# Half of the softmax tiles of a hybrid encoder block turned by VectorE and DMA instead of TensorE, with the source's order on all engines

## The chip, the cores and the metric

One core of a Trainium2 chip runs the kernel. The metric is the device time of one execution in microseconds; lower is better. The engines are TensorE (PE, matrix products; PEld is its loading of weights), VectorE (DVE), ScalarE (ACT), GpSimd (POOL) and SyncE (SP), which here only issues DMAs. DMAs can also be issued from ScalarE's queue. On-chip data lie in SBUF with 128 partitions; TensorE writes to PSUM, from where VectorE or ScalarE read.

## The reference

One layer over 512 positions of width 2048:

- `mod = silu(c) @ w_cond + b_cond` gives shift, scale and gate; `h = rms_norm(x) * (1 + scale) + shift`.
- `proj = h @ w_in` (7200 columns) is cut into attention queries, keys, values and gate (1024 each), the queries, keys, values and gate of a gated linear attention (512, 512, 1024, 1024) and two low-rank gates (16 each).
- Attention: 16 heads of width 64, three dilated window patterns whose outputs are merged with weights from their softmax denominators:

```
s = einsum(q, k) / 8 + bias[bucket]; s = where(mask, s, -1e30)
p = exp(s - max); den = sum(p); o = (p / den) @ v; lse = max + log(den)
att = sum over patterns of softmax(lse) * o
```

- Linear attention: 4 heads, chunked scans forward and backward, summed, normalised.
- `y = concat(att * silu(gate_a), gla * silu(gate_g)) @ w_out`; the result is `rms_norm(x + gate * y) * final_gain`.

## The kernel before

Everything is float32. A product is made exact enough by splitting both sides into a high and a low part (float32r) and summing three products: `three(ps, lh, ll, rh, rl)` issues high × high, low × high, high × low, each a matmul of 128×128 by 512 columns. The three dilated patterns are one softmax over all 512 keys: a row of biases per head (`grow`, in DRAM) holds the T5 bias plus the log of how many patterns see a distance.

After a start that computes `h` and the first products, the kernel runs **units**: qk2, qk4, qk6, gk, gv0, gv1, ag0, ag1, gg0, gg1, o0 to o3. A unit makes 512 columns of a projection: 8 weight groups g (two 128-row blocks of 512 columns each, one DMA of 512 KB), and in each group four output tiles of two products, so 64 **ticks** of `three`. Its four accumulators (`PJ`) come from five PSUM buffers; three more (`PA`) serve everything else. The weights of a group are loaded into one of four `raw` buffers (`fetch`), split by ScalarE into a high part (`split_hi`) and by VectorE into a low part (`split_lo`); three buffers hold each part. At the start of a group, the code splits the next group and fetches two ahead; `upto` says how far.

Between the ticks a unit carries **side work**, a list of (position from 0 to 1, function). A position of 1 or more is carried into the next unit. For qk2, qk4, qk6 and gk it is attention over two pairs of heads (`attention(pairs)`), 16 tiles of 128 queries each:

- `score(h, i)`: two matmuls make 128 queries × 512 keys in PSUM; VectorE adds the bias and takes the minimum, ScalarE exponentiates with the sum, VectorE inverts the sum, GpSimd scales: the tile `p`.
- `turn(h, i)`: TensorE transposes `p` in four 128×128 blocks into PSUM; ScalarE takes the high part, VectorE the low one.
- `values(h, half)`: eight matmuls with the turned tiles of two `i`; ScalarE and VectorE put the two rows of sums together in `cat`.

At the end of qk2, qk4 and qk6, `qk_evict` reads the four finished accumulators for the two pairs of heads that the next unit will need: per pair four ScalarE and four VectorE instructions and four DMAs on SP that copy keys to the other 64 partitions.

Further side work are the **sums** (`some_sums`): 48 loads of 512 KB and VectorE reductions over them for the gate and for a bias; `SUMS_IN` says how many each unit carries.

TensorE runs in the source's order throughout (`tc.manual_schedule(engines={E.PE})`). In the start, the other engines run in an order planned by `_plan` (with `manual_schedule(engines=PLANNED)`, where PLANNED are GpSimd, VectorE, ScalarE and SyncE). In all units after it the tile scheduler orders those four engines; side work is marked a little more urgent (`urgent`, an offset of 20).

Of the kernel before, what the change touches and what calls it, by code (L numbers as in the profile page):

```python
# [72 lines left out]
ATT_AT = (0.17, 0.8, 0.04, 0.05, 0.05)  # L73
# [4 lines left out]
SUMS_IN = {"qk6": 4, "gk": 4, "gv0": 9, "gv1": 2, "ag0": 7, "ag1": 9, "gg0": 9}  # L78
# [55 lines left out]
def block_kernel(ctx: ExitStack, tc: tile.TileContext, a: dict):  # L134
# [421 lines left out]
    def attention(pairs):  # L556

        tiles = [(2 * p + j, i) for p in pairs for j in range(2) for i in range(4)]
        gt, pt, pr_ = {}, {}, {}
        heads = [2 * p + j for p in pairs for j in range(2)]  # L560

        def g_load(h):
            g = gp.tile([P, 896], F32, tag="g", name=f"g{h}")
            nc.sync.dma_start(g, bass.AP(grow.tensor, grow.offset + h * 1024, [[1, P], [1, 896]]))
            gt[h] = g

        def score(h, i):
            def go():
                if h % 8 == 0 and i == 0:
                    cat[h // 8] = B8(f"cat{h // 8}", [4, 512])  # L570
# [12 lines left out]
                act(t, t, AF.Exp, bias=st[:, 0:1], scale=-1.0, accum_out=st[:, 1:2])  # L583
                nc.vector.reciprocal(st[:, 2:3], st[:, 1:2])  # L584
# [4 lines left out]
        def turn(h, i):  # L589
            def go():  # L590
# [7 lines left out]
                hi = pt[h, half][:, 0, :, P * ii:P * ii + P]  # L598
                lo = pt[h, half][:, 1, :, P * ii:P * ii + P]
# [4 lines left out]

        def values(h, half):
            def go():
                t = pt.pop((h, half))
# [15 lines left out]
        for x in range(n + 4):  # L623
            if x < n:
                items.append(score(*tiles[x]))
            if 2 <= x <= n + 1:
                items.append(turn(*tiles[x - 2]))
            if 3 <= x <= n + 2 and tiles[x - 3][1] % 2 == 1:
                items.append(values(tiles[x - 3][0], tiles[x - 3][1] // 2))
        g_load(heads[0])  # L630
        start, span, move0, move1, move_last = ATT_AT
        at = [start + (q + 0.5) / len(items) * span for q in range(len(items))]
        at[0] -= move0
        at[1] -= move1
        at[-1] += move_last
        return list(zip(at, items))
# [206 lines left out]
    def unit(name, natural, side=(), rhs=None, lr=None, tiles=range(4)):  # L843
# [5 lines left out]
        for q in range(KT // 2):  # L849
            g = gorder[q] if name == "o3" else q  # L850
            i0 = gi[name, g]
            todo = []
            if 0 in tiles:
                todo = list(range(gi[name, gorder[0] if name == "o3" else 0], upto[name, g] + 1))
# [4 lines left out]
            if i0 not in low:  # L859
                split_lo(i0)  # L860
            hi, lo = wts[i0]
            for n, i in enumerate(tiles):
                for kk in range(2):
                    k = 2 * g + kk
                    rh, rl = (h_hi[:, k, :], h_lo[:, k, :]) if rhs is None else rhs[k]
                    if natural:
                        t = slice(i * P, i * P + P)
                        cw = slice(kk * 512, kk * 512 + 512)
                        three(ps[n], rh[:, t], rl[:, t], hi[:, cw], lo[:, cw], q + kk == 0, q + kk == KT // 2)
                    else:  # L870
                        c = slice(kk * 512 + i * P, kk * 512 + i * P + P)
                        three(ps[n], hi[:, c], lo[:, c], rh, rl, q + kk == 0, q + kk == KT // 2)
                    tick += 1
                    if tick % (2 * len(tiles)) == 2:
                        for i_ in todo:
                            split_lo(i_)
                    while pos < len(side) and side[pos][0] * ticks <= tick:
                        urgent(side[pos][1])
                        pos += 1
                if lr is not None:  # L880
                    lr(4 * g + i)
# [18 lines left out]
    for p in range(2):  # L900
        qk_evict(p, psb["b", 4 + 2 * p], psb["b", 5 + 2 * p])
    for n, p in (("qk2", 0), ("qk4", 2), ("qk6", 4)):
        ps = unit(n, False, attention((p, p + 1)) + ([(0.05, shift_row)] + some_sums(n) if p == 4 else []))
        for q in range(2):
            qk_evict(p + 2 + q, ps[2 * q], ps[2 * q + 1])

    ps = unit("gk", False, attention((6, 7)) + some_sums("gk"))
    gla["k"] = B8("gkt", [4, 512])
    for i in range(4):
        act(gla["k"][:, i, :], ps[i], AF.Copy)  # L910


    lrb = B8("lrb", [KT, 32])
    nc.sync.dma_start(lrb, a["w_lr"][0])
    lrs = B8("lrs", [KT, 2, 32], F32R)
    act(lrs[:, :, 0, :], lrb, AF.Copy)
    tt(lrs[:, :, 1, :], lrb, lrs[:, :, 0, :].bitcast(F32), op=ALU.subtract)
    plr = PA("plr")

    def lr_tick(n):  # L920
        if n % 2 == 1:
            k = n // 2
            w = lrs[:, k, :, :].rearrange("p a b -> p (a b)")
# [207 lines left out]
```

## Time and profile before

| | us |
|---|---|
| median of 3 runs | 958.9 (958.15 to 960.98) |
| the profiled execution | 959.9 |
| its span, first to last instruction | 957.9 |
| TensorE busy | 939.7 (98%) |
| VectorE busy | 605.3 (63%) |
| ScalarE busy | 431.5 (45%) |
| GpSimd busy | 81.1 (8%) |

The span is what the profile sees; the profiled execution took 2.0 us more. TensorE's busy time counts a pipelined matmul from its start to its modelled end, so consecutive matmuls overlap: a 512-column matmul has 0.39 us, but the next starts 0.23 us later. The chain of waits counts each instruction only from the end of the one before. A group row gives line, engine, operation, output and inputs, shapes, count, then busy us and the mean ns of one, and the idle time of that engine ahead of these instructions with what ended it. A timeline row gives start, duration, engine, line, operation, tiles and in brackets the idle time ahead. A row of DMA issues gives the size and the median time from issue to landing.

### The profile page before, as it was taken

The numbers are of one execution on the slowest core, as the hardware profiler recorded it, in microseconds if no ns is written. First come the engines' busy times: TensorE is split into PE (matmuls) and PEld (weight loads), VectorE is DVE, ScalarE is ACT, GpSimd is POOL, SyncE is SP. The second block draws the span as 40 slices with busy tenths as digits, with TensorE's granted clock in tenths as the row PEclk, the third lists the DMA queues.
The fourth block names the chain that finished last, engine by engine and source line by source line (L and its number), as shares of the span: only waits on it lengthen the run. The fifth ranks groups of instructions, "written<-read, shape, count | busy, mean of one in ns | idle before, by whom it ended". The sixth has DMA issues, their size and how long they took to land.

```text
span 957.9 us, 11999 instructions
## 1 busy us (share of the span) xinstructions
PE 939.7 (98%) x4464; PEld 777.1 (81%) x4464; DVE 605.3 (63%) x900; ACT 431.5 (45%) x719; POOL 81.1 (8%) x100
## 2 busy tenths in 40 slices
PE   8999999999999999999999999999999999999996
PEld 5888788888888888888778888888887888888884
DVE  7988899675756676766435656675964352546421
ACT  5443533565655655655215544543834152233222
POOL 0000000012122022122000000000010000202120
PEclk9999999999999999999999999999999999999998
DMA  9999687443333463533454244354555464244013
GB/s 330 413 411 365 229 296 275 150 131 105 112 103 105 144 200 108 173 127 103 150 176 146 86 132 154 132 176 154 173 195 183 132 221 154 92 151 152 23 55 121
DMA packets 45180, 163.76 MB, mean 171 GB/s; under 512 B 5730, under 2 KB 6018, under 8 KB 40386
## 3 DMA queue, kind: packets, MB, share of 16 engines
q1 hardware_dynamic: 44946, 162.68, 49.9%
q8 instruction: 35, 0.57, 0.2%
q10 hardware_dynamic: 176, 0.33, 0.1%
q14 instruction: 23, 0.18, 0.1%
HBM read 154.51 MB, written 4.28 MB: 166 GB/s over the span
## 4 chain that ended last, share of the span: by engine, by line
PE 84%; DMA 6%; DVE 5%; issue 3%; ACT 1%; SPq 0%; POOL 0%; ACTq 0%; DVEq 0%; POOLq 0%
PE ps_o L170 6%; PE ps_o L169 6%; PE ps_o L171 6%; DMA rawg<-in_wg 6%; PE ps_qk L170 5%; PE ps_qk L169 5%; PE ps_qk L171 5%; PE o L611 3%; PE sta L169 3%; PE sta L170 3%; PE sta L171 3%; PE stb L171 3%; PE stb L169 3%; PE stb L170 3%; PE ps_gv L171 3%; PE ps_gv L170 3%
## 5 line engine op out<-in xcount | busy, mean ns | idle before, releaser
L585 POOL TENSOR_SCALAR p<-p,st 128x512 f32<-128x512 f32 x64 | 45.5, 711 | 406.6 <-DVE st L584 357.9
L244 DVE CUSTOM_DVE_ANT_0 cb<-cb,sb,c_bcond 128x2048 f32<-128x2048 f32 (+1 forms) x32 | 73.4, 2294 | 0.0
L583 ACT ACTIVATE p<-p,st 128x512 f32<-128x512 f32 x64 | 46.1, 721 | 56.8 <-DVE st L580 56.3
L602 DVE TENSOR_TENSOR pt<-t,pt 128x512 fp32r<-128x512 f32 x64 | 44.0, 689 | 16.2 <-ACT pt L601 15.8
L580 DVE CUSTOM_DVE_ANT_0 p<-s,g 128x512 f32<-128x512 f32 x64 | 43.6, 687 | 14.8 <-PE s L577 14.5
L601 ACT ACTIVATE pt<-t 128x512 fp32r<-128x512 f32 x64 | 37.8, 592 | 10.2 <-PE t L597 9.2
L244 DVE CUSTOM_DVE_ANT_0 rawg<-rawg,sb,gate 128x1024 f32<-128x1024 f32 x16 | 20.5, 1283 | 29.6 <-DMA rawg<-in_wg 29.6
L611 PEld LDWEIGHTS o<-pt,vv 128*128 128x128 f32 x256 | 34.7, 188 | 5.0 <-DVE pt L602 2.2
L597 PEld LDWEIGHTS t<-c_ident,p 128*128 128x128 f32 x256 | 31.8, 140 | 8.5
L597 PE MATMUL t<-c_ident,p 128*128 128x128 f32 x256 | 38.3, 272 | 0.0
L611 PE MATMUL o<-pt,vv 128*128 128x256 f32 x256 | 36.6, 283 | 0.9 <-DVE pt L602 0.8
L244 DVE CUSTOM_DVE_ANT_0 rawg<-rawg,sb,c_bcond 128x1024 f32<-128x1024 f32 x16 | 20.5, 1283 | 26.3 <-DMA rawg<-in_wg 26.3
L1014 POOL TENSOR_TENSOR x<-x,fgain 128x512 f32<-128x512 f32 x12 | 20.3, 1696 | 185.3 <-ACT ysq L1012 185.3
L1012 ACT ACTIVATE ysq<-x 128x512 f32<-128x512 f32 x16 | 10.1, 632 | 47.2 <-DVE x L1010 47.2
L767 POOL TENSOR_SCALAR dc<-st,sc 128x256 f32<-128x256 f32 x16 | 10.4, 652 | 245.5 <-DVE st L764 240.6
L1009 DVE TENSOR_TENSOR y<-ps_o,sb 128x512 f32<-128x512 f32 x16 | 10.9, 684 | 25.9 <-PE ps_o L171 25.9
L584 DVE RECIPROCAL st<-st 128x1 f32<-128x1 f32 x64 | 10.3, 162 | 24.9 <-ACT p L583 24.9
L576 PE MATMUL s<-ks,qs 128*128 128x512 f32 x64 | 25.1, 391 | 0.0
L577 PE MATMUL s<-kl,qs 128*128 128x512 f32 x64 | 25.0, 391 | 0.0
L774 ACT ACTIVATE sq<-st,sc 128x256 f32<-128x256 f32 x24 | 12.2, 509 | 26.8 <-DVE st L769 14.3
L1010 DVE TENSOR_TENSOR x<-y,x 128x512 f32<-128x512 f32 x16 | 18.0, 1125 | 0.3
L614 ACT ACTIVATE oh<-o 64x256 f32<-64x256 f32 x32 | 12.2, 382 | 13.0 <-PE o L611 12.2
(1275 smaller groups left out, 2916.7 us busy)
## 6 DMA issues: line engine op xcount, KB each, us to landing
cb<-in_wm SPq DMA_DIRECT2D x31, 1024.0 KB, 7.9
rawg<-in_wg SPq DMA_DIRECT2D x32, 512.0 KB, 3.4
raw_o<-in_w_o SPq DMA_DIRECT2D x32, 512.0 KB, 3.4
raw_qk<-in_w_qk SPq DMA_DIRECT2D x24, 512.0 KB, 3.4
rawb<-in_w_sb SPq DMA_DIRECT2D x16, 512.0 KB, 4.8
rawv<-in_wv SPq DMA_DIRECT2D x16, 512.0 KB, 3.8
raw_gv<-in_w_gv SPq DMA_DIRECT2D x16, 512.0 KB, 3.5
raw_ag<-in_w_ag SPq DMA_DIRECT2D x16, 512.0 KB, 3.3
```

Of the source, the lines that this page charges most:

```text
L169: mm(ps, lh, rh, start=first, stop=False)
L170: mm(ps, ll, rh, start=False, stop=False)
L171: mm(ps, lh, rl, start=False, stop=last)
L244: nc.vector.tensor_tensor_reduce(out=w, in0=w, in1=with_, op0=ALU.mult, op1=ALU.add, scale=1.0, scalar=init, accum_out=dst)
L576: mm(ps, qs[:, q], ks, start=True, stop=False)
L580: nc.vector.tensor_tensor_reduce(out=t, in0=ps, in1=gt[h][:, P * i:P * i + 512], op0=ALU.add, op1=ALU.min, scale=1.0, scalar=3e38, accum_o ...
L583: act(t, t, AF.Exp, bias=st[:, 0:1], scale=-1.0, accum_out=st[:, 1:2])
L585: nc.gpsimd.tensor_scalar(t, t, st[:, 2:3], 1.0, op0=ALU.mult, op1=ALU.mult)
L597: nc.tensor.transpose(pk[:, kt * P:kt * P + P], t[:, kt * P:kt * P + P], ident)
L601: act(hi, src, AF.Copy)
L602: tt(lo, src, hi.bitcast(F32), op=ALU.subtract)
L611: mm(po[:, :256], vv[h // 4][:, kt, h % 4, :], t[:, w, kt, :], start=kt == 0 and w == 0, stop=kt == 3 and w == 1)
```

## The change

Attention: each head has four query tiles in two halves. Half 0 (tiles 0 and 1) no longer goes to TensorE. VectorE's transpose turns the 32×32 blocks within the tile (`turn`), two DMAs store the tiles to DRAM (`leave`), four DMAs read them back so that the blocks come to lie in their places (`back`, into a `raw` buffer), and ScalarE and VectorE split the half into a high part (`part_hi`) and a low part (`part_lo`), 128×1024 each. Half 1 is turned by TensorE as before (`pe_turn`). Every step has its own position in units of tiles (`x + 1.1` and so on), spaced by `ATT_AT`; the last steps fall into the next unit.

The region from the first `qk_evict` to the end of gv0 stands in `manual_schedule(engines=PLANNED)`: ScalarE, VectorE, GpSimd and SyncE issue in the order of the source there.

In the units of q, k and gk, weights are fetched on ScalarE's queue, as are the bias tiles (`g_load`). These units handle groups 0 and 1 as one step: tile by tile, both groups. Eight sums leave qk6 and gk for gv0, gv1, ag0 and gg1. The low-rank weights are loaded and split during gk.

```diff
-ATT_AT = (0.17, 0.8, 0.04, 0.05, 0.05)
+ATT_AT = (0.12, 0.057)
+BY_DVE = (0,)
+BACK_AT = (2.7, 4.1, 4.4, 5.6)
-SUMS_IN = {"qk6": 4, "gk": 4, "gv0": 9, "gv1": 2, "ag0": 7, "ag1": 9, "gg0": 9}
+SUMS_IN = {"gv0": 12, "gv1": 5, "ag0": 8, "ag1": 9, "gg0": 9}
...
-            nc.sync.dma_start(raws[i], a["w_" + u][g])
+            queue = nc.scalar if u[:2] in ("qk", "gk") else nc.sync
+            queue.dma_start(raws[i], a["w_" + u][g])
...
+        def turn(h, i):
+            def go():
+                t = T2(f"pt{h}{i}")
+                nc.vector.transpose(t.rearrange("p (b k r) -> p k b r", b=4, k=4), pr_.pop((h, i)))
+                pr_[h, i] = t
+            return go
+        def leave(h, i):
+            def go():
+                half, ii = divmod(i, 2)
+                if ii == 0:
+                    away[h, half] = dp.tile([2, P, 512], F32, tag=f"away{h}{half}", name=f"away{h}{half}")
+                nc.sync.dma_start(away[h, half][ii], pr_.pop((h, i)))
+            return go
+        def back(h, half):
+            def go():
+                t = away.pop((h, half))
+                f = RAW(f"pf{h}{half}", [8, 128])
+                for b in range(4):
+                    nc.sync.dma_start(f[32 * b:32 * b + 32], bass.AP(
+                        t.tensor, t.offset + P * b, [[512, 32], [32 * 512, 8], [1, P]]))
+                pf[h, half] = f
+            return go
+        def part_hi(h, half):
+            def go():
+                t = pt[h, half] = B8(f"pt{h}{half}", [2, 4, 256], F32R)
+                src = pf[h, half].rearrange("p b (k r) -> p k b r", k=4)
+                act(t[:, 0].rearrange("p k (b r) -> p k b r", b=8), src, AF.Copy)
+            return go
...
+        for x in range(n):
+            h, i = tiles[x]
+            items.append((x, score(h, i)))
+            items.append((x + 0.75, scale(h, i)))
+            half, ii = divmod(i, 2)
+            if half in BY_DVE:
+                items.append((x + 1.1, turn(h, i)))
+                items.append((x + 1.5, leave(h, i)))
+                if ii:
+                    for at, piece in zip(BACK_AT, (back, part_hi, part_lo, values)):
+                        items.append((x + at, piece(h, half)))
+            else:
+                items.append((x + 1.8, pe_turn(h, i)))
+                if ii:
+                    items.append((x + 2.9, values(h, half)))
+        start, step = ATT_AT
+        return [(start + step * x, go) for x, go in items]
...
+        steps = [order_[:2]] if name[:2] in ("qk", "gk") else [order_[:1], order_[1:2]]
+        for step in steps + [[g] for g in order_[2:]]:
...
+                todo = list(range(gi[name, order_[0]], upto[name, step[-1]] + 1))
                 for i in todo:
                     split_hi(i)
                 for ahead in (1, 2):
-                    fetch(upto[name, g] + ahead)
+                    fetch(upto[name, step[-1]] + ahead)
+            for g in step:
+                split_lo(gi[name, g])
             for n, i in enumerate(tiles):
+                for g in step:
...
+    with tc.manual_schedule(engines=PLANNED):
+        for p in range(2):
+            qk_evict(p, psb["b", 4 + 2 * p], psb["b", 5 + 2 * p])
+        for n, p in (("qk2", 0), ("qk4", 2), ("qk6", 4)):
+            ps = unit(n, False, attention((p, p + 1)) + ([(0.6, shift_row)] if p == 4 else []))
+            for q in range(2):
+                qk_evict(p + 2 + q, ps[2 * q], ps[2 * q + 1])
```

More of the change, by code (lines that the diff above doesn't have):

```diff
@@ L622, in attention @@
         n = len(tiles)
[L623 to L629, printed above, removed]
-        g_load(heads[0])
[L631 to L636, printed above, removed]
+        for x in range(n):
[13 more added lines that the diff above has]
+                    items.append((x + 2.9, values(h, half)))
+        items.sort(key=lambda v: v[0])
+        g_load(heads[0])
+        start, step = ATT_AT
+        return [(start + step * x, go) for x, go in items]
     def gate_half(m, z):
@@ new lines, in unit @@
+                for g in step:
+                    hi, lo = wts[gi[name, g]]
+                    for kk in range(2):
+                        k = 2 * g + kk
+                        rh, rl = (h_hi[:, k, :], h_lo[:, k, :]) if rhs is None else rhs[k]
+                        first, last = (g, kk) == (order_[0], 0), (g, kk) == (order_[-1], 1)
+                        if natural:
+                            t = slice(i * P, i * P + P)
+                            cw = slice(kk * 512, kk * 512 + 512)
+                            three(ps[n], rh[:, t], rl[:, t], hi[:, cw], lo[:, cw], first, last)
+                        else:
+                            c = slice(kk * 512 + i * P, kk * 512 + i * P + P)
+                            three(ps[n], hi[:, c], lo[:, c], rh, rl, first, last)
+                        tick += 1
+                        if tick % (2 * len(tiles)) == 2:
+                            for i_ in todo:
+                                split_lo(i_)
+                        while pos < len(side) and side[pos][0] * ticks <= tick:
+                            urgent(side[pos][1])
+                            pos += 1
+                    if lr is not None:
+                        lr(4 * g + i)
@@ L897, in gate_evict @@
         lnexp()
[L900 to L910, printed above, removed]
```

85 lines of the change are left out of this document (39 added, 46 removed).

## The prediction

> **What bounds the kernel now.** I read the page's busy table first, then the stretches of the five projection units that the change touches, then the chain of waits inside one of them.
>
> ```profile
> span 957.9 us, 11999 instructions
> PE 939.7 (98%) x4464; PEld 777.1 (81%) x4464; DVE 605.3 (63%) x900; ACT 431.5 (45%) x719; POOL 81.1 (8%) x100
> ```
> ```profile
> 191.87:257.29 65.42, 65.39 (x345) 54.91 (x344) 43.49 (x90) 38.84 (x75) 11.15 (x16) 1.00 0.37 113
> 257.29:323.71 66.42, 66.39 (x353) 55.91 (x352) 41.95 (x89) 37.43 (x72) 11.17 (x16) 1.00 0.36 108
> 390.28:457.51 67.23, 66.39 (x353) 55.92 (x352) 45.01 (x94) 36.50 (x70) 12.05 (x16) 1.00 0.42 132
> 457.51:510.39 52.88, 52.51 (x233) 41.21 (x232) 20.14 (x26) 12.15 (x15) 0.00 (x0) 1.00 0.46 150
> ```
> The stretches are the units qk2, qk4, gk and gv0 (length, then PE, PEld, DVE, ACT, POOL busy, granted clock, DMA share, GB/s). TensorE is busy in all but 0.03 us of qk2 and of qk4, 0.84 of gk and 0.37 of gv0. So a microsecond taken from TensorE's list there is a microsecond won, and a microsecond for which TensorE waits is lost: there is no slack to hide it in.
>
> ```profile
> 204.04 0.23 PE ps_qk L171
> 204.27 0.44 PE t L597 x4
> 204.71 0.23 PE ps_qk L169
> 210.68 0.94 PE o L611 x8
> ```
> In the chain one 512-column matmul counts 0.23 us (a tick of three 0.68), four transposes 0.44, the eight matmuls of a "values" step 0.94. Unit qk2 is made of 192 × 0.2267 = 43.5, 16 scores of two matmuls 7.3, 16 turns 7.0 and 7 values 6.6 (the eighth falls into the next unit): 64.4 of the measured 65.4. The remaining 1.0 I spread over its 23 interruptions, 0.04 each.
>
> **The change part by part.**
>
> *Half of the turns leave TensorE.*
> ```profile
> L597 PE MATMUL t<-c_ident,p 128*128 128x128 f32 x256 | 38.3, 272 | 0.0
> L602 DVE TENSOR_TENSOR pt<-t,pt 128x512 fp32r<-128x512 f32 x64 | 44.0, 689 | 16.2 <-ACT pt L601 15.8
> L580 DVE CUSTOM_DVE_ANT_0 p<-s,g 128x512 f32<-128x512 f32 x64 | 43.6, 687 | 14.8 <-PE s L577 14.5
> L585 POOL TENSOR_SCALAR p<-p,st 128x512 f32<-128x512 f32 x64 | 45.5, 711 | 406.6 <-DVE st L584 357.9 <-PE t L597 16.2 <-PE s L576 10.8
> ```
> 256 transposes are 64 turns; 32 go: 32 × 0.44 = 14.1 us, and 32 × 0.04 = 1.3 of the interruptions. **−15.4**, all on the path.
>
> *What replaces them, off the path if on time.* Each of 32 tiles gets a block transpose by VectorE. No row shows one; by the nearest ones below it costs between 0.48 (128x256) and 1.22 us (a scan of 128x512); I take 0.69, the two-input 128x512 row above, since it walks the same 512 columns once.
> ```profile
> L432 DVE SCALAR_TENSOR_TENSOR vv<-vraw,rcol,vv 128x256 fp32r<-128x256 f32 x16 | 6.7, 479 | 0.0
> L717 DVE TENSOR_TENSOR_SCAN b<-rst,g 128x512 f32<-128x512 f32 x4 | 4.9, 1225 | 0.1
> L297 DVE TENSOR_TENSOR qk41l<-raw_qk,qk41h 128x1024 fp32r<-128x1024 f32 x1 | 1.2, 1222 | 0.0
> ```
> The split of 128x512 twice (2 × 0.69) becomes one of 128x1024 (1.22). Per unit VectorE gains 8 × 0.69 − 4 × 0.16 = +4.9 us: 43.5 to 48.4 in a unit of about 62. Covered at 0.69 and, at 1.22, still below the unit (52.6).
>
> *The round trip.* Per half of a head: two stores of 256 KB, then four loads of 128 KB that wait on SP for the stores.
> ```profile
> g<-grow SPq DMA_DIRECT2D x16, 448.0 KB, 4.4
> out<-x SPq DMA_DIRECT2D x16, 256.0 KB, 2.6
> ks<-ks SPq DMA_DIRECT2D x16, 128.0 KB, 2.2
> ```
> ```profile
> 256.65 0.46 SPq L549 DMA_DIRECT2D ks<-ks  x1
> ```
> One attention step is 0.057 of a unit, 3.5 us. Counted from a score: matmuls 0.45, VectorE 0.7, ScalarE 0.7, POOL 0.71 and handovers make p ready at about 3.4; VectorE turns it behind the next score's work, done at 5.6; store 2.6: 8.2. The loads go out from 2.7 steps or then, four issues of 0.46, the last landing 2.2 (like ks) to 4.4 (like g) later: 11.8 to 14.0. The high part is asked for at 4.1 steps, 14.4. Nominally on time, **0** on the path; queued behind it on SP are only the next stores and loads, since the weights of these units have moved to ScalarE's queue. The 16.8 MB go into units whose DMA share is 0.36 to 0.5.
>
> *Source's order on all engines.* This is where I see the loss. The timelines at the end of qk2 (ScalarE, then VectorE, then TensorE):
> ```profile
> 248.92 1.06 ACT L313 ACTIVATE qk41h<-raw_qk 128x1024 fp32r<-128x1024 f32 x1 [0.95 <-PE ps_qk L171]
> ...
> 256.03 0.59 ACT L548 ACTIVATE ks<-ps_qk 64x512 fp32r<-64x512 f32 x1
> 256.64 0.59 ACT L539 ACTIVATE qs<-ps_qk 64x512 fp32r<-64x512 f32 x1
> ...
> 267.00 0.72 ACT L583 ACTIVATE p<-p,st 128x512 f32<-128x512 f32 x1 [2.02 <-DVE st L580]
> ...
> 267.72 0.71 ACT L583 ACTIVATE p<-p,st 128x512 f32<-128x512 f32 x1
> ```
> ```profile
> 256.76 0.69 DVE L550 TENSOR_TENSOR kl<-ps_qk,ks 64x512 fp32r<-64x512 f32 x1
> ...
> 270.14 0.69 DVE L580 CUSTOM_DVE_ANT_0 p<-s,g 128x512 f32<-128x512 f32 x1 [1.43 <-PE s L577]
> ```
> ```profile
> 257.29 0.39 PE L169 MATMUL ps_qk<-h_hi,qk40h 128*128 128x512 f32 x1
> ...
> 263.71 0.39 PE L169 MATMUL ps_qk<-h_hi,qk41h 128*128 128x512 f32 x1
> ...
> 269.60 0.39 PE L577 MATMUL s<-kl,qs 128*128 128x512 f32 x1
> ```
> Before, group 1 of qk4 is split at 248.9, 8.4 us ahead of the unit, between the evictions, and TensorE needs it 6.4 us into the unit. After, the source emits the split of group 1 only at the new unit's start, behind `qk_evict` of both pairs; and TensorE, which now takes groups 0 and 1 tile by tile, needs it after two ticks. Let 0 be the issue end of the old unit's last matmul. The last score (step 15, 0.12 + 15 × 0.057 = 0.975, tick 63 of 64) has its second matmul at −0.91. By the rows VectorE starts 0.54 later (269.60 to 270.14), −0.37, and takes 0.70; ScalarE's exp is done 0.72 after 0.37, at 1.09. Then eight evictions 0.61 apart (256.03 to 256.64): 5.97. The high part of group 1: 7.0. VectorE's eight eviction steps of 0.69, each behind ScalarE's, end at 7.45; the low part, 1.22: 8.7. TensorE has two ticks and one turn, 1.36 + 0.44 = 1.8, issues one matmul when the high part comes, and would have started the second at 2.0: **6.7 lost**. Then the turn of tile 15 waits: VectorE does group 2's low part first (to 10.0), reciprocal, POOL 0.71: 10.9, where TensorE arrives at 10.5: 0.4. Together 7.1 at each of three borders (qk2/qk4, qk4/qk6, qk6/gk): **+21.3**. Bounds for one border: 3.5 (if only the last pair's two k evictions, 1.2, 1.4 of VectorE and the split stood behind the end) and 9 (if issuing g's load and the two fetches held ScalarE as well). At gk/gv0 there are only four evictions and group 1 isn't needed for eight ticks: nothing; the 0.84 and 0.37 us idle of gk and gv0 come from the old order there and may go: **−1.2**.
>
> *The clock.* TensorE would stand still from 1.8 to 7.0, 5.2 us. The end and the start of this trace show what that does:
> ```profile
> 948.22 0.39 PE L171 MATMUL ps_o<-o36l,c_h 128*128 128x512 f32 x1
> ```
> ```profile
> 951.00:952.00 1.00, 0.00 (x0) 0.00 (x0) 0.58 (x1) 0.94 (x3) 0.45 (x1) 1.00 0.00 0
> 952.00:953.00 1.00, 0.00 (x0) 0.00 (x0) 0.17 (x1) 0.75 (x2) 0.73 (x1) 0.65 0.00 0
> ```
> ```profile
> 12.67 0.80 PE L170 MATMUL sta<-sa0h,h_lo 128*128 128x512 f32 x1
> ...
> 15.40 0.63 PE L170 MATMUL sta<-sa0h,h_lo 128*128 128x512 f32 x1
> 15.83 0.63 PE L171 MATMUL sta<-sa0l,h_hi 128*128 128x512 f32 x1
> ```
> ```profile
> 17.32 0.39 PE L169 MATMUL sta<-sa0h,h_hi 128*128 128x512 f32 x1
> 17.55 0.40 PE L170 MATMUL sta<-sa0h,h_lo 128*128 128x512 f32 x1
> ```
> The last matmul ends at 948.6; the granted clock falls at about 952.3 (0.65 over that microsecond), 3.7 us later. At the start dense matmuls go every 0.43 us from 12.67 to about 17.0 and 0.23 after: 4.3 us at half rate, 2.0 lost. An idle time of 5.2 is above 3.7, but one observation doesn't say that it happens each time: I take two of three borders, **+4.0**, bounds 0 and 6. [...]
>
> *Sums moved.*
> ```profile
> L244 DVE CUSTOM_DVE_ANT_0 rawg<-rawg,sb,gate 128x1024 f32<-128x1024 f32 x16 | 20.5, 1283 | 29.6 <-DMA rawg<-in_wg 29.6
> ```
> Eight sums leave qk6 and gk; gv0 and gv1 get three more each, ag0 and the last gate unit one. 3 × 1.28 = 3.9 us on a VectorE busy 20 of 53 us in gv0: 0, bounds −1 and +3 (if a late load holds the weight splits behind it). The early load of the low-rank weights is in the −1.2.
>
> **Sum.** The profiled execution took 959.9 (span 957.9 and 2.0 around). 959.9 − 15.4 + 21.3 − 1.2 + 4.0 = 968.6; it stands 1.0 above the median of the three runs, 958.9, so **968**, 0.9% slower.
>
> **Rivals.**
> *The border is short (faster).* The gain is 16.6; three borders cost as much at 5.5 us each, clock included. If ScalarE and VectorE reach group 1 soon after the last tile, at 3.5 a border and no drop of the clock: 958.9 − 16.6 + 10.5 = 953; with no stall at all 942. For it: the operands are on chip in time (raw weights are fetched a whole group ahead), and ScalarE is only 56% busy (37.4 of 66.4 us). Against: the eviction of the last tile can't begin before 0, and emission order puts all eight behind the last exp.
> *About no change.* A border of 5.5, or 7.1 without the clock and with a further 3 us of spared interruptions: 956 to 962.
> *The steady state stalls as well.* In source order VectorE's list for one head (four scores 0.69, two turns, two plus one splits, weight splits 1.22 twice, merges) is 10.7 of 14 us, and each item waits for its place: the merge of one half stands behind the next tile's score, and a score's PSUM buffer (three in all) behind the merge. Decides if a head loses over 0.3 us; at 0.8 per head, 16 heads: +13, 981. For it the low slack of the round trip, 0.4 us at its slow bound. [...]
> *It does not do what it says:* TensorE's turns stay at 64. Excluded by the source, no chance given.
>
> **How the numbers follow.** Border stall as worked out 0.47 (968; own range 962 to 975), short border 0.24 (953), about no change 0.14 (959), steady stalls too 0.15 (981). A measurement of this kernel can tell about 0.3%, 2.9 us, from no change. Short border counts as faster with a part of the third case; faster 0.25, same 0.13, slower 0.62. The range 951 to 980 leaves out the no-stall end (a tenth) and the worst of the steady stalls (a tenth).
>
> **What would show it.** 32 × 4 transposes on TensorE; qk2 near 62 us, qk4, qk6 and gk near 69; TensorE idle 5 to 7 us in front of the first matmul with group 1, released by ScalarE's high part and then VectorE's low part of qk41, qk61, gk1; matmuls every 0.43 us behind some of these gaps. Wrong if those gaps are under 5 us, or if idle time is spread over the turns and values, released by part_lo or by loads of pf.

## The result: 4.0% slower, and the profile after

The changed kernel takes 998.2 us (median; 996.7 to 998.8) against 959.0 for the kernel before on the same chip: ratio 1.040, 95% interval 1.038 to 1.042. The sign and the place were forecast, the size was not: 39 us lost instead of 9, beyond the forecast's 951 to 980.

The page of the changed kernel, its span and its busy table:

```profile
span 997.0 us, 11866 instructions
PE 937.9 (94%) x4336; PEld 771.8 (77%) x4336; DVE 620.9 (62%) x917; ACT 428.1 (43%) x704; POOL 78.9 (8%) x100
```

TensorE has 128 matmuls fewer (32 × 4: the turns did leave it). It is now idle for 59 us of the span (997.0 − 937.9), against 18 before. The stretches of the units qk2, qk4, qk6, gk and gv0 (columns as in the prediction):

```profile
192.98:260.12 67.14, 62.20 (x297) 51.10 (x296) 40.24 (x83) 31.07 (x59) 9.96 (x15) 0.97 0.56 168
260.12:337.30 77.18, 66.02 (x321) 54.53 (x320) 45.49 (x93) 36.68 (x68) 11.08 (x17) 0.93 0.52 147
337.30:415.00 77.70, 66.50 (x322) 55.13 (x321) 45.49 (x93) 36.85 (x69) 11.07 (x17) 0.91 0.56 159
415.00:492.72 77.72, 66.84 (x321) 55.22 (x320) 45.53 (x93) 37.32 (x70) 10.87 (x16) 0.91 0.54 147
492.72:549.10 56.38, 54.14 (x248) 42.70 (x247) 29.81 (x43) 16.82 (x24) 1.38 (x2) 1.00 0.67 227
```

qk4 and gk, each of which begins with a border behind a qk unit, are 10.8 and 10.5 us longer than before, qk6 11.1 and qk2 1.7. The stretch given for gv0 leaves out its last two matmuls (gv1 begins at 549.56); with them gv0 is 4.0 longer. The border qk2/qk4 in the timelines of TensorE, ScalarE and VectorE:

```profile
261.49 0.60 PE L608 MATMUL t<-c_ident,p 128*128 128x128 f32 x4
270.59 0.79 PE L173 MATMUL ps_qk<-h_hi,qk41h 128*128 128x512 f32 x1 [8.50 <-ACT qk41h L318]
271.85 0.79 PE L174 MATMUL ps_qk<-h_hi,qk41l 128*128 128x512 f32 x1 [0.47 <-DVE qk41l L302]
272.44 0.63 PE L175 MATMUL ps_qk<-h_lo,qk41h 128*128 128x512 f32 x1
272.87 0.63 PE L173 MATMUL ps_qk<-h_hi,qk41h 128*128 128x512 f32 x1
...
284.97 0.36 PE L665 MATMUL o<-pt,vv 128*128 128x256 f32 x1 [1.61 <-DVE st L583]
```
```profile
261.26 0.59 ACT L544 ACTIVATE qs<-ps_qk 64x512 fp32r<-64x512 f32 x1
262.60 0.59 ACT L544 ACTIVATE qs<-ps_qk 64x512 fp32r<-64x512 f32 x1 [0.75 <-DVE qs L545]
...
264.67 0.59 ACT L553 ACTIVATE ks<-ps_qk 64x512 fp32r<-64x512 f32 x1 [0.86 <-DVE kl L555]
...
266.80 0.59 ACT L544 ACTIVATE qs<-ps_qk 64x512 fp32r<-64x512 f32 x1 [0.92 <-DVE qs L545]
...
268.86 0.59 ACT L553 ACTIVATE ks<-ps_qk 64x512 fp32r<-64x512 f32 x1 [0.86 <-DVE kl L555]
...
269.48 1.06 ACT L318 ACTIVATE qk41h<-raw_qk 128x1024 fp32r<-128x1024 f32 x1
...
281.90 1.06 ACT L647 ACTIVATE pt<-pf 128x1024 fp32r<-128x1024 f32 x1 [4.78 <-DMA pf<-away]
```
```profile
269.49 0.69 DVE L555 TENSOR_TENSOR kl<-ps_qk,ks 64x512 fp32r<-64x512 f32 x1 [0.66 <-ACT ks L553]
270.57 1.23 DVE L302 TENSOR_TENSOR qk41l<-raw_qk,qk41h 128x1024 fp32r<-128x1024 f32 x1 [0.39 <-ACT qk41h L318]
...
282.99 1.22 DVE L654 TENSOR_TENSOR pt<-pf,pt 128x1024 fp32r<-128x1024 f32 x1 [5.15 <-ACT pt L647]
284.13 0.68 DVE L583 CUSTOM_DVE_ANT_0 p<-s,g 128x512 f32<-128x512 f32 x1
```

Read from the bottom up. TensorE stops behind the turn at 261.49, as forecast; it would have gone on at 261.93 and gets the high part of group 1 at 270.59, then waits for the low part. That is 8.66 + 1.03 = 9.7 us by the starts. ScalarE comes to the split of group 1 at 269.48 because the eight evictions stand ahead of it and four of them wait for VectorE's read of the same accumulator: 0.75 + 0.86 + 0.92 + 0.86 = 3.4 us. Behind the gap the matmuls go every 0.43 us. At 284.97 a values step waits once more. It is released by VectorE's step for a score (L583, 284.13). That stands behind the low part of the turned half (L654, 282.99), which VectorE makes only after ScalarE got its data at 281.90. Why these data were late shows in SP's timeline:

```profile
270.21 0.46 SPq L556 DMA_DIRECT2D kl<-kl  x1
271.82 3.32 SPq L638 DMA_DIRECT2D pf<-away  x4
```

The loads of a turned half stand on SP behind the key copies, which wait for the evictions. They go out 1.1 us after the last copy's issue has ended, at 271.82, because they need a `raw` buffer, and VectorE's split of group 1 (270.57 to 271.80, above) frees it: SP's wait for `qk41l` is 1.1 us, and the same 1.1 at the two borders after it. Behind these three borders the loads then took 6.5 to 8.8 us to land. On the page, the groups that the change added or made wait:

```profile
L665 PE MATMUL o<-pt,vv 128*128 128x256 f32 x256 | 36.7, 286 | 6.3 <-DVE st L583 5.7
L654 DVE TENSOR_TENSOR pt<-pf,pt 128x1024 fp32r<-128x1024 f32 x16 | 19.6, 1225 | 30.4 <-ACT pt L647 30.4
...
L608 PE MATMUL t<-c_ident,p 128*128 128x128 f32 x128 | 19.8, 278 | 4.4 <-POOL p L595 4.4
L620 DVE STREAM_TRANSPOSE pt<-p 128x512 f32<-128x512 f32 x32 | 22.7, 709 | 0.8 <-POOL p L595 0.7
pf<-away SPq DMA_DIRECT2D x64, 128.0 KB, 3.2
```

### The profile page after: what moved, and what is told of

It is laid out like the page before. It is cut to its first block, busy times and chain, and to the rows that moved or that the text cites. A ratio compares the mean times of both kernels' runs of the same rounds, so it can differ in the third digit from the quotient of the medians.

```text
span 997.0 us, 11866 instructions
## 1 busy us (share of the span) xinstructions
PE 937.9 (94%) x4336; PEld 771.8 (77%) x4336; DVE 620.9 (62%) x917; ACT 428.1 (43%) x704; POOL 78.9 (8%) x100
## 4 chain that ended last, share of the span: by engine, by line
PE 42%; DMA 8%; DVE 5%; issue 2%; ACT 2%; SPq 0%; ACTq 0%; POOL 0%; DVEq 0%; POOLq 0%
PE ps_o L173 6%; PE ps_o L174 6%; PE ps_o L175 6%; PE ps_gg L173 3%; PE ps_gg L174 3%; PE ps_gg L175 3%; DMA rawg<-in_wg 3%; DMA pf<-away 2%; DMA rawv<-in_wv 2%; PE ps_gv L174 2%; PE ps_gv L173 2%; PE ps_gv L175 2%; PE ps_ag L175 1%; PE ps_ag L174 1%; PE ps_ag L173 1%
## 5 line engine op out<-in xcount | busy, mean ns | idle before, releaser
L583 DVE CUSTOM_DVE_ANT_0 p<-s,g 128x512 f32<-128x512 f32 x64 | 43.6, 681 | 1.5 <-PE s L580 1.1
L654 DVE TENSOR_TENSOR pt<-pf,pt 128x1024 fp32r<-128x1024 f32 x16 | 19.6, 1225 | 30.4 <-ACT pt L647 30.4
L612 DVE TENSOR_TENSOR pt<-t,pt 128x512 fp32r<-128x512 f32 x32 | 22.0, 686 | 17.8 <-ACT pt L611 17.7
L611 ACT ACTIVATE pt<-t 128x512 fp32r<-128x512 f32 x32 | 19.1, 596 | 16.4 <-PE t L608 15.9
L647 ACT ACTIVATE pt<-pf 128x1024 fp32r<-128x1024 f32 x16 | 16.8, 1050 | 18.1 <-DMA pf<-away 18.1
L608 PE MATMUL t<-c_ident,p 128*128 128x128 f32 x128 | 19.8, 278 | 4.4 <-POOL p L595 4.4
L608 PEld LDWEIGHTS t<-c_ident,p 128*128 128x128 f32 x128 | 16.2, 144 | 9.8 <-POOL p L595 5.7
L620 DVE STREAM_TRANSPOSE pt<-p 128x512 f32<-128x512 f32 x32 | 22.7, 709 | 0.8 <-POOL p L595 0.7
```

The lines of the kernel that those rows point to most:

```text
L583: nc.vector.tensor_tensor_reduce(out=t, in0=ps, in1=gt[h][:, P * i:P * i + 512], op0=ALU.add, op1=ALU.min, scale=1.0, scalar=3e38, accum_o ...
L608: nc.tensor.transpose(pk[:, kt * P:kt * P + P], t[:, kt * P:kt * P + P], ident)
L620: nc.vector.transpose(t.rearrange("p (b k r) -> p k b r", b=4, k=4), pr_.pop((h, i)))
```

## The experiments: order or turning?

The first three kernels take one of the two main parts away each, or the trip's waits. The runs were made on several chips, on which the kernel before took 957.5 to 959.0 us. Each ratio is to the kernel before on the same chip; two kernels on different chips that lie less than some 3 us apart are not told apart.

**Order of the other engines.** The region of written order becomes the scheduler's; TensorE's own order stays.

```diff
-    with tc.manual_schedule(engines=PLANNED):
+    if True:
         for p in range(2):
             qk_evict(...)
```


> The changed kernel (998.2 us) without the region that puts ScalarE, VectorE, GpSimd and SyncE into the source's order from the first eviction to the end of gv0; everything else of the change stays. If the order is the cause (three borders of 9.7 us idle and 2.1 to 3.2 us at half rate), the split of group 1 is done ahead of the evictions again and the borders close: 945 to 965 us. If the round trip through DRAM is the cause, whatever the order: 980 us or more.

963.0 us, 1.005 (1.003 to 1.007): 35 of the 39 us are back. The order is the main cause, yet the turning by VectorE has won nothing against the kernel before.

**All turns by TensorE, source's order.**
```diff
-BY_DVE = (0,)
+BY_DVE = ()
```


> The changed kernel with all turns by TensorE (no tile goes through DRAM), in the same source order. If the order is the cause, the borders stay (8 to 10 us idle each) and the removed turns come back, +14 to +15 us, less what the round trip costs (the waits of the values step behind the borders, 2.0 to 2.6 us each, and about 1 elsewhere): 1000 to 1010 us. If the round trip is the cause: 960 to 975 us.

999.5 us, 1.044 (1.041 to 1.046): 15 us more work on TensorE cost 1 us, 3 by the ratios. Its list isn't the bound when the other engines hold the source's order: the gap at the border shrinks from 8.50 to 7.53 us, and values no longer wait there.

**No trip.** The four loads read the input instead of the stored tiles, so they wait for no store; the probabilities of these halves are left out.
```diff
+                    x_ = a["x"]
                     nc.sync.dma_start(f[32 * b:32 * b + 32], bass.AP(
-                        t.tensor, t.offset + P * b, ...
+                        x_.tensor, x_.offset + P * b, ...
```


> The changed kernel whose four loads per half read 128 KB pieces of the input x instead of the tiles just stored, so they wait for no store (the stores stay; the probabilities of half of the queries are left out of the result). If the border's order is the cause, only the waits behind the loads go (values behind the border, 2.0 to 2.6 us each): 990 to 996 us. If the wait of the loads for the stores is the main cost: 970 us or less.

999.7 us, 1.044 (1.042 to 1.045): neither of the two outcomes expected. The waits of values stay (1.79, 2.18 and 1.51 us behind the borders), so the loads' wait for the stores is not on the path. What remains is their place behind the evictions.

## The experiments: inside the border

**Group 1 split earlier.** The last group's step of a qk unit also splits group 1 of the next unit, ahead of the evictions.
```diff
+more = name[:2] == "qk" and step[-1] == order_[-1]
-todo = list(range(gi[name, order_[0]], upto[name, step[-1]] + 1))
+todo = list(range(gi[name, order_[0]], upto[name, step[-1]] + 1 + more))
```


> The changed kernel with one edit: the last group step of qk2, qk4 and qk6 also splits group 1 of the next unit, so that the splits stand in the source ahead of the evictions. If the border's order is the cause: the idle gap before the first matmul with group 1 goes; but the turn of the last tile still waits for its reciprocal behind the eight evictions (at 272.3 us instead of the 275.4 now reached), so 3 to 4 us per border are won, 9 to 12 in all: 986 to 990 us. If something else in the unit is the cause: 995 to 999 us.

1001.2 us, 1.046 (1.044 to 1.047): no gain, where 9 to 12 us were expected. TensorE's timeline at the same border:

```profile
264.73 0.50 PE L173 MATMUL ps_qk<-h_hi,qk40h 128*128 128x512 f32 x1 [1.23 <-DVE qs L545]
273.52 1.12 PE L608 MATMUL t<-c_ident,p 128*128 128x128 f32 x4 [7.83 <-POOL p L595]
285.58 1.30 PE L665 MATMUL o<-pt,vv 128*128 128x256 f32 x8 [3.43 <-DVE st L583]
```

The wait for qk41 is gone and 7.83 us stand at the next thing that sits behind the evictions: the turn of the last tile, whose reciprocal (L594) VectorE reaches only after them.

**The evictions alternate between the two accumulators** (q, k, q, k in place of q, q, k, k).
```diff
 act(qs[own], psq[own, ::-1], AF.Copy, scale=-0.125)
+act(ks[own], psk[own], AF.Copy)
 stt(qs[oth], psq[own, ::-1], -0.125, qs[own].bitcast(F32), ...)
-stacks[2 * p + j] = [qs, None, None, own]
 ...
```


> The changed kernel with the eviction of a pair written so that ScalarE and VectorE work on different accumulators in turn (q, k, q, k instead of q, q, k, k); the same instructions. The eviction of two pairs took 8.9 us in the changed kernel (261.26 to 270.18) because each second ScalarE read of an accumulator waited 0.75 to 0.9 us for VectorE's read of the same one; with the reads alternating, VectorE's eight steps should follow each other, 6.2 to 6.5 us. If the eviction's length sets the idle gap at the border, the gap falls from 8.8 to 6 to 6.5 us at three borders and 2 to 2.5 us are won at the start of qk2 as well: 0.8 to 1.1 % faster than the changed kernel, 987 to 990 us. If the gap is set by something else: no change.

989.6 us, 1.034 (1.031 to 1.037), as expected. Of the four waits at this border two are left, shorter, in ScalarE's timeline:

```profile
261.99 0.59 ACT L546 ACTIVATE qs<-ps_qk 64x512 fp32r<-64x512 f32 x1 [0.27 <-DVE qs L548]
...
264.87 0.59 ACT L546 ACTIVATE qs<-ps_qk 64x512 fp32r<-64x512 f32 x1 [0.48 <-DVE qs L548]
```
```profile
267.31 0.79 PE L173 MATMUL ps_qk<-h_hi,qk41h 128*128 128x512 f32 x1 [5.84 <-ACT qk41h L318]
```

The idle falls from 8.50 to 5.84, 2.7 us at each of three borders, and the kernel by 8.5 us. With the waits nearly gone the gap has about the size of the forecast (5.2).

**Early split, and steps begin earlier**, so that the last reciprocal comes ahead of the evictions: the edit of the early split and
```diff
-ATT_AT = (0.12, 0.057)
+ATT_AT = (0.10, 0.057)
```


> The changed kernel with group 1 split in the unit before, and all attention positions 0.02 of a unit earlier, so that the reciprocal of the last tile stands ahead of the evictions too. If what is behind the evictions in the source's order is the whole border loss, TensorE now waits only for accumulators (1.5 to 2 us, then up to 2 more): 26 to 33 us are won, 964 to 972. If a further item waits there (the loads of the last half, behind the key copies on SP), 980 to 990.

981.1 us, 1.025 (1.022 to 1.027): 17 us back, where the early split alone won nothing. The earlier start alone wasn't tried. Now values wait 3.68 us there.

**All border edits**: this kernel, alternating evictions, and the third weight group fetched ahead of the first evictions (`fetch(2)` at the start of the region).

> The run before plus the alternating eviction and the load of qk2's group 2 issued ahead of the first evictions. If the border theory holds throughout: no gap over 2 us at the borders, qk2 at 61 to 63 us, the four units at 62 to 65 each: 945 to 955 us, faster than the kernel before (957.6). If the round trip limits the steady state: 960 to 975.

965.1 us, 1.007 (1.005 to 1.009). qk2 falls from 67.1 to 60.0 us. What is left in TensorE's timeline:

```profile
261.69 0.36 PE L661 MATMUL o<-pt,vv 128*128 128x256 f32 x1 [1.04 <-DVE pt L608]
263.33 1.86 PE L661 MATMUL o<-pt,vv 128*128 128x256 f32 x7 [1.28 <-DVE pt L608]
```

**The gap filled with work.** Forty extra matmuls stand ahead of group 0 in qk4, qk6 and gk (the real ones restart the sum), so that TensorE doesn't stand still at the border.
```diff
+if name in ("qk4", "qk6", "gk") and step[0] == 0:
+    for _ in range(40):
+        mm(ps[0], wts[gi[name, 0]][0][:, :P], h_hi[:, 0, :], start=True, stop=True)
```


> The changed kernel with 40 further matmuls of 0.2267 us (9.1 us) at the start of qk4, qk6 and gk, into an accumulator that the unit overwrites afterwards. They stand where TensorE idles for 8.8 us, so they cost 0 to 1 us per border in themselves. If the idle time halves the clock and so costs 2.1 to 3.2 us per border behind it, the half-rate matmuls vanish: 990 to 993 us. If the half rate were no consequence of the idle time: 998 to 1001 us.

1001.9 us, 1.047 (1.044 to 1.049), above both times expected. The matmuls behind keep 0.23 us, but the next wait grows by what they win:

```profile
271.41 0.50 PE L174 MATMUL ps_qk<-h_hi,qk41l 128*128 128x512 f32 x1 [0.47 <-DVE qk41l L302]
271.75 0.39 PE L175 MATMUL ps_qk<-h_lo,qk41h 128*128 128x512 f32 x1
...
284.05 1.76 PE L665 MATMUL o<-pt,vv 128*128 128x256 f32 x8 [3.24 <-DVE st L583]
```

3.24 instead of 1.61 us. Behind this wait the clock falls after all: the matmuls from 285.61 to 287.31 go every 0.43 us, and so at all three borders. In the changed kernel too they do so behind the values of qk6 and gk. Within a unit the values come out at about the same time in both (24.4 and 24.9 us after the start of qk4). So the slow clock at the border was real and was covered by the wait for the turned half. The filling only moved it, and the time without any slow clock was not measured.

## The experiments: what the turning is worth, and a third cause

**The repaired border with all turns by TensorE** (`BY_DVE = ()`).

> The repaired border (last group step also splits the next unit's group 1, reciprocals and spilled steps earlier, alternating evictions, third weight tile fetched ahead of the first evictions: 965.1 us) with all 64 turns by TensorE. Theory A (the turning takes 15 us from TensorE's list, and the waits of values steps for parts that come late give most of them back): TensorE's list grows by 15.4, the waits of about 3 us at each of three borders and the 1.6 of clock behind them go, some 10 to 12 together: 968 to 971. Rival B (the list of TensorE is off the path even with the border repaired, as it was under the order of the changed kernel, where it made 1 us): 965 to 967. Rival C (nothing is given back by the turning): 980.

977.1 us, 1.021 (1.017 to 1.024): between theory A and rival C. Turning by VectorE is worth 12.0 us once the border is closed.

**The repaired border with parts and values a step later.**
```diff
-BACK_AT = (2.7, 4.1, 4.4, 5.6)
+BACK_AT = (2.7, 5.1, 5.4, 6.6)
```


> The same repaired border, turning as in the changed kernel, with the high part, low part and values of a turned half one step later (BACK_AT 2.7, 5.1, 5.4, 6.6; the loads stay where they are). Theory A (what is left at the borders, 1.4 to 1.6 us twice each and half rate behind it, is values waiting for a low part that came late by a few us): three and a half us of slack close it, 965 - 8 = 957, and values show no wait over 0.6. Rival D (VectorE and ScalarE are late at the border as a whole, and anything that stands in their order waits as long): 964 to 966, the waits now at turns, scores or the next values.

974.8 us, 1.017 (1.014 to 1.020): worse than either theory has it. Behind the border at 326.8 values still wait, 1.84 + 1.28 us, and now also at the unit's end (0.87) and in gv0 (3.57). Each of the five units is 1.9 to 3.1 us longer than with the repaired border; why isn't followed further.

**The scheduler's order with all turns by TensorE.** This leaves only the small parts of the change.

> The scheduler's order in place of the source's, and all 64 turns by TensorE: the changed kernel without its two main parts (left are the weights on ScalarE's queue, two groups tile by tile at the start of a unit, the moved sums). Theory A (under the scheduler's order the turning by VectorE gave back as much as it took): 960 to 964, like the 963.0 with turning. Rival E (the turning wins there, 8 us or more, and the other parts cost that): 971 or more. Rival F (the turning itself is the loss, the rest costs nothing): 957 to 959, the time of before.

976.5 us, 1.019 (1.015 to 1.024): rival E. The turning wins 13.4 us under this order too (963.0), and what is left of the change costs 18. TensorE's timeline at the border names one:

```profile
268.83 0.47 PE L579 MATMUL s<-ks,qs 128*128 128x512 f32 x1 [1.44 <-DMA ks<-ks]
271.39 0.79 PE L580 MATMUL s<-kl,qs 128*128 128x512 f32 x1 [2.09 <-DMA kl<-kl]
```

The first score of a new pair waits for the copies of its keys. In the kernel before, the first copy left at 254.94, 2.3 us ahead of the unit's start, and the first score came at 264.39, 7.1 us after it. Here TensorE is ready for the score 7.3 us after the start (259.88), but the first copy leaves at 263.15, 3.3 us after it.

**The scheduler's order with parts and values a step later** (the same `BACK_AT`).

> The scheduler's order, turning by VectorE for half, with the high part, low part and values one step later (BACK_AT 2.7, 5.1, 5.4, 6.6). With BACK_AT as it was it took 963.0, with waits of 1.7 to 3.5 us in front of values at four borders and 1.26 behind three of them, some 14 us. Theory A (these waits are slack that lacked): 950 to 955, faster than before. Rival D (the late parts are late in any order, because VectorE, ScalarE and the transfers crowd there): 961 to 964.

958.1 us, 0.999 (0.998 to 1.001): the waits of values at the border went (5 us won), those of the first score for kl, the low part of the keys, stayed (2.55 us at qk4).

**The scores begin later and closer together**, on top of that.
```diff
-ATT_AT = (0.12, 0.057)
+ATT_AT = (0.19, 0.051)
```


> The scheduler's order, turning by VectorE for half, parts and values a step later (that was 958.1 us), and the scores of a pair begin later and closer together: ATT_AT (0.19, 0.051) for (0.12, 0.057). Theory K (the first score of a pair comes before the copies of its keys have landed: 2.55 us of waiting for kl, 0.3 to 2.3 around it and 1.2 to 2.2 of half rate behind, at three borders 14 us by the trace with 0.12): a start 3.1 us later takes 8 to 14 off, 944 to 950, faster than before; no score waits for kl over 0.6. Rival (transfers, VectorE and ScalarE are as late whatever is asked when, and the wait goes to the next values): 956 to 960.

**946.1 us, 0.9885 (0.9871 to 0.9900): faster than both kernels.** The score no longer waits, and the units qk2 to gv0 have these stretches:

```profile
265.19 0.40 PE L579 MATMUL s<-ks,qs 128*128 128x512 f32 x1
265.42 0.40 PE L580 MATMUL s<-kl,qs 128*128 128x512 f32 x1
```
```profile
191.70:252.97 61.27, 60.13 (x302) 50.52 (x300) 41.66 (x86) 34.08 (x62) 12.13 (x16) 1.00 0.54 152
252.97:316.31 63.34, 62.73 (x324) 52.89 (x322) 45.94 (x93) 37.77 (x70) 13.90 (x17) 1.00 0.60 171
...
443.93:497.78 53.85, 53.85 (x247) 42.65 (x246) 29.25 (x40) 14.97 (x22) 0.13 (x1) 1.00 0.70 229
```

qk2 and qk4 are 4.2 and 3.1 us shorter than before. In ScalarE's and SP's timelines one sees what the scheduler did with the border at 252.97: group 1 split 8.4 us ahead of it, the loads of the turned half ahead of the key copies.

```profile
244.53 1.06 ACT L318 ACTIVATE qk41h<-raw_qk 128x1024 fp32r<-128x1024 f32 x1 [1.26 <-PE ps_qk L175]
```
```profile
252.71 1.80 SPq L638 DMA_DIRECT2D pf<-away  x4
255.51 0.47 SPq L554 DMA_DIRECT2D ks<-ks  x1
```

**The same start of the scores, all turns by TensorE, scheduler's order.**

> The scheduler's order, all turns by TensorE (that was 976.5 us), and ATT_AT (0.19, 0.051). What is left of the change beside the time of the scores are the weights on ScalarE's queue, two groups tile by tile and the moved sums. Theory K (early scores are the third part of the loss: stalls of 2.1, 3.9, 4.2 and 3.7 us in qk2, qk4, qk6 and gk with 4.7 of half rate, 18.5 together): 958 to 962, the time of before. Rival (the weights on ScalarE's queue or the two groups cost it): 970 to 976.

957.2 us, 1.000 (0.999 to 1.001): the time of before. So the times of the attention steps (`ATT_AT`) were the 18 us, and the weights on ScalarE's queue, the two groups tile by tile and the moved sums together cost nothing here. The key copies still leave after the unit's start (258.61, it starts at 256.70), and the first score now comes 11.4 us after it. Why the scheduler evicts later than in the kernel before isn't told apart.

**The source's order, repaired border, later scores and values** (`ATT_AT = (0.17, 0.05)`, values at 6.4 and 4.5).

> The source's order with the repaired border (965.1 us), scores later and closer (ATT_AT (0.17, 0.05) for (0.10, 0.057)), values a step later (6.4 and 4.5 for 5.6 and 2.9), so that neither the keys nor the spilled values are asked for before ScalarE and VectorE have done the evictions. Theory (what was left at a border, 0.85 + 1.44 + 1.64 and 2.1 of half rate, 6 each at three, is asked too early): 947 to 953. Rival (the source's order makes ScalarE and VectorE late whatever is asked when): 962 or more.

983.2 us, 1.027 (1.025 to 1.028), a miss. The turns now wait (3.14 us at 258.50 for GpSimd's product): with the early split ahead of them on VectorE and scores closer together, the last reciprocals are late again.

**The weights back on SP's queue**, the changed kernel otherwise.
```diff
-queue = nc.scalar if u[:2] in ("qk", "gk") else nc.sync
+queue = nc.sync
```


> The changed kernel with all weights loaded by SP's queue, as before the change; its other parts kept. Theory (the border chain, the early scores and not the queue are the loss; only group 2 of qk2, fetched late on ScalarE's queue behind the evictions, was the queue's, some 3 to 5 us, and on SP the weights stand behind loads that wait for stores instead): 993 to 1003. Rival (ScalarE's issues of 0.33 to 0.45 us and its order hold the weights up in every unit): 985 or less.

994.9 us, 1.040 (1.038 to 1.042): 3 us less than the changed kernel, but the same ratio to the kernel before, so no gain is shown. In its trace values idle 1.9 us behind the borders instead of 5.7. Group 2 of qk2 is as late (a wait of 2.85 us), since on SP its load stands behind the key copies: the place in the order makes it late, not the queue.

**The order alone.** The kernel of 946.1 us with the source's order, differing in that one line (TensorE keeps the source's order in both).

> The source's order of the changed kernel with ATT_AT (0.19, 0.051) and BACK_AT (2.7, 5.1, 5.4, 6.6): it differs from the kernel that took 946.1 us by the order on the engines alone. Theory B (the border chain stands whatever the scores do: eight evictions and the split of group 1 behind the old unit's last matmul, 8 to 10 us at each of three borders, and half rate behind them): 985 to 995, with gaps of 7 us or more in front of the first matmul with the high part of qk41, qk61 and gk1. Rival K (the early scores were the larger cause under this order too): 955 to 965.

998.9 us, 1.041 (1.039 to 1.044), above the 985 to 995 expected, with the gap where it was:

```profile
270.70 0.79 PE L173 MATMUL ps_qk<-h_hi,qk41h 128*128 128x512 f32 x1 [8.85 <-ACT qk41h L318]
271.96 0.79 PE L174 MATMUL ps_qk<-h_hi,qk41l 128*128 128x512 f32 x1 [0.47 <-DVE qk41l L302]
```

The order of VectorE, ScalarE, GpSimd and SP costs 52.8 us (51.4 if each kernel is taken against the kernel before on its chip). The later scores, worth 12 to 19 us under the scheduler's order (958.1 to 946.1, 976.5 to 957.2), and the later parts are worth nothing under the source's: another wait stands ahead of theirs.

## Why the prediction was wrong, step by step

**The turns leave TensorE: −15.4. Right, as a bound.** 128 matmuls went. Where nothing else stood on the path it was worth 11.1 (957.2 to 946.1), 12.0 and 13.4 us; the rest went mostly into waits of values for their parts (3.5 us in the trace of the 946.1 kernel). The block transpose took 0.709 us against 0.69 taken, the part of 128x1024 1.225 against 1.22.

**The border: place right, size wrong. This is the step that failed**: "Then eight evictions 0.61 apart: 5.97." The 0.61 came from a k eviction followed by a q eviction, two accumulators. In the source's order ScalarE reads the same accumulator twice running, and the second read waits for VectorE's read of it. By the rows above, with 0 at 260.12, the evictions begin at 1.14 (1.09 forecast), the high part is done at 10.4 (7.0 forecast), and the 3.4 between are the four waits. 9.7 lost per border in place of 6.7: 9 us of the miss of 30; the alternating evictions gave 8.5 back. The 0.4 at the turn behind it did not come. The wait stood in the trace of before, in ScalarE's timeline:

```profile
253.13 0.59 ACT L539 ACTIVATE qs<-ps_qk 64x512 fp32r<-64x512 f32 x1 [0.52 <-DVE qs L540]
```

ScalarE's second read and the VectorE read that it waits for are of different halves of 64 partitions. The wait of 0.75 to 0.92 us is there all the same, so in this program it seems to go by the accumulator.

**What else stood behind the evictions: left out.** The forecast saw the split and the turn of the last tile there. It missed three things. The loads of the turned half: "queued behind it on SP are only the next stores and loads" looked at what they hold up, not at what holds them: the key copies, and the `raw` buffer that the split of group 1 frees. Values idled 6.3 us in all, where the forecast had nothing. The weights of qk2's third group, asked for behind the first evictions:

```profile
205.91 1.06 ACT L318 ACTIVATE qk22h<-raw_qk 128x1024 fp32r<-128x1024 f32 x1 [6.63 <-DMA raw_qk<-in_w_qk]
```

TensorE waited 1.63 and 0.76 us for their high and low part and 2.01 for a turn behind them, and qk2 became longer by 1.7 in place of shorter by 3.9. And the spilled steps in gv0, which became 4.0 longer; the forecast had gk and gv0 together 1.2 shorter.

**The clock: seen, but not a cost.** Every border went to half rate (0.91 to 0.93 granted in these units, matmuls 0.43 us apart behind the gaps), more often than the two of three taken. Filling the gap suggests that the +4.0 wasn't to be added: another wait stood behind it. The same holds for each border wait by itself. The granted clock fell 4.5, 2.4 and 3.2 us after the last matmul ahead of the three gaps of 8.5 us (the prediction had 3.7 from the end of the kernel before).

**The round trip: 0, right inside a unit.** The loads took 3.2 us in the median (2.2 to 4.4 taken), and without their wait for the stores nothing changed. Behind the borders it was not 0: the loads took 6.5 to 8.8 us there, see the values above.

**A ledger of the profiled executions**, span against span: −15.4 for the turns; 3 × 9.7 = 29.1 at the borders; 6.3 at values; 5.6 for qk2 (+1.7 in place of −3.9); 4.0 for gv0; and by the starts of matmuls further apart than 0.23 us, 2.1 + 2.4 + 3.2 = 7.7 of half rate in the three units behind the gaps. That is 37.3 of 39.1 (997.0 − 957.9). Against the forecast, term by term: 9.0 from the evictions, −1.2 from the turn's wait that did not come, 6.3 from values, 5.6 from qk2, 5.2 from gv0 (4.0 in place of −1.2) and 3.7 from the clock (7.7 in place of 4.0), 28.6 of the 30 missed. These are no sizes of what a repair returns: each wait covers others.

**Rivals.** "The steady state stalls as well" (981) came nearest, for another reason: not every head, but what the border makes late. "Short border" was excluded by the order. The change of `ATT_AT` was taken as a place on a time line and not as an edit with a price of its own; under the scheduler's order it cost 19 us with all turns by TensorE. Under the source's order the later start won nothing (998.9), so it isn't a part of this miss.

## What to carry to other kernels

In an order written out by hand, list for each engine and queue everything that comes behind a burst at a border (splits, reciprocals, loads, copies, the buffers that these free), and take the first wait that such a burst shows in the trace, not its bare instruction time: here the removal of one late item uncovered the next (7.83 us at the turn after the early split). Let evictions alternate between accumulators (8.5 us here). Work taken from the busiest engine pays only once order and start times fit it: here the same turning by VectorE went with 39 us lost or 11 won (998.2 and 946.1).

## What was not expected of the hardware

**The clock fell at no fixed time after the matmuls stopped.** In the scheduler's order with TensorE's turns, dense matmuls ended at 267.4, one came at 268.83 for 0.47 us, and the granted clock (the column behind POOL) fell at about 269.7, 2.3 us after the dense ones:

```profile
269.20:269.60 0.40, 0.10 (x1) 0.00 (x0) 0.00 (x0) 0.00 (x0) 0.00 (x0) 1.00 1.12 256
269.60:270.00 0.40, 0.00 (x0) 0.00 (x0) 0.00 (x0) 0.00 (x0) 0.00 (x0) 0.60 1.03 190
```

At the end of the kernel before it was 3.7 us, with no matmul in between. With the repaired border, dense matmuls ended at 260.7, one came at 261.69 for 0.36 us, and the granted clock fell at about 262.4, 1.7 us after the dense ones. With its parts a step later, they ended at 334.0, one came at 335.80 for 0.36 us, the seven from 337.44 took 1.86 us (1.10 at 325.88), and the matmuls from 339.10 on went every 0.43 us. These three falls came with no 3.7 us of idle time ahead of them.

The changed kernel shows different times with no matmul in the pause. At its three borders the clock fell 4.5, 2.4 and 3.2 us after the last matmul. Ahead of values TensorE paused for 1.61 us in qk4, and the granted clock stayed at 1.00. A pause of 2.22 us in qk6 and one of 1.89 us in gk were followed by a fall, at about 362.1 and 440.6, 2.5 and 3.0 us after the pauses began, when matmuls already ran again. What decides, and how little work is enough, isn't told apart.
